# Head 0's mixes at fixed places among the reads of scores, its v loaded behind the next head's q, and the last logarithm ahead of other casts

## The chip, the core and the metric

One NeuronCore of a Trainium2 chip runs the whole program. The time is the device's, in microseconds of one execution. The kernel of before took 965.34, 965.65 and 966.77 us in three runs, a median of 965.65. Its profiled execution took 964.64 us.

A core has five engines, each with its own queue of instructions: TensorE (PE in the profile: matmuls and transposes; PEld is its loading of weights), VectorE (DVE), ScalarE (ACT), GpSimd (POOL) and SyncE (SP, which here only issues DMAs). They meet through semaphores. Matmuls write to banks of PSUM, which DVE and ACT read.

## The reference, cut to what matters

One layer on 1024 tokens of width 1024: norm, a wide projection `w_in`, two groups of heads side by side, a projection `w_out`, norm, residual. The change touches the eight heads of differential attention and the norm of their output:

```python
def block(args):                       # 128 queries, one head
    s = jnp.einsum('bqhmd,bkhmd->bhmqk', qb, k)          # two maps, m = 0, 1
    p = jax.nn.softmax(jnp.where(mask, s, -jnp.inf), axis=-1)
    w = p[:, :, 0] - lam * p[:, :, 1]
    return jnp.einsum('bhqk,bkhv->bqhv', w.astype(v.dtype), v)

oa = diff_attention(qa, ka, va, lam)                     # 8 heads, d = 64, v of 128
oa = rms_norm(oa, subln_g) * (1.0 - lam_init)
oa = oa * jax.nn.silu(ga)
y = jnp.concatenate([oa, ob]) @ w_out                    # ob: the other group
return x + rms_norm(y, post_g)
```

## The kernel before

The in-projection runs first and stores q, k and v of all heads to DRAM (q and k in a high and a low part, from tiles `qk_st`, `qk_hi` and `c`, L482). Attention follows, at about 617 us of the span, and the out-projection is laid between its matmuls: `merge` at the end of the program zips three streams, `all_scores`, `all_values` and `out_early`, by planned costs into one program. A scheduler then orders each engine's instructions by priority and dependence, except those under `tc.keep_in_program_order` (they keep their order among each other) and `tc.issue_after(x)` (behind instruction x).

**Scores.** `scores(h, qb)` makes one block of 128 queries, for `qb` from 7 down to 0, of `n = (qb + 1) * 128` keys. For each of the two maps m it takes the keys in parts of up to 512: PE multiplies q with k and with its low part ks into one of three score banks in rotation (`sc_bank`), and DVE reads the bank, adds the mask, writes the scores to the map's tile (p0 or p1) and their extreme value to `st`. This read is the row `CUSTOM_DVE_ANT_0` of the profile, `ISA` in the lists of the order; the short row behind it fetches the reduced value. In the text a read is named by block and map: block 6's second map has a read of 512 and one of 384 keys. After a map's last read ACT takes the exponential in place with row sums into `st`. After the second map DVE takes the reciprocal of both sums, POOL scales p1 by lambda over its sum, and DVE mixes: `p0 = p0 / sum0 - p1` (`mix_maps`, `SCALAR_TENSOR_TENSOR p<-p,stt,p` in the profile). p0 has a buffer for each block, p1 two in all.

In head 0 the mixes of blocks 7 to 4 are put off: each is put into the list `mixed` and issued behind the last read of the next block, which the scheduler is then free to place. The reciprocals and the reads are free too.

**Values.** `turn` transposes the mixed weights on PE into a bank `wtr`, ACT casts them to `wt_hi`, DVE takes the rest `wt_lo`; `weigh` multiplies them with v into the bank `po` (L142). Head h's v comes in two loads of 512 KB each, by SP (L1243). Head 0's are issued at the program's start of the attention, kept in program order, in tiles taken from the pool `smp` ahead of all others; those of the next heads follow when the head before has ended its first half. q, k and ks of head h + 1 are loaded by SP when head h has reached block 4 (L1127, L1130).

**Norm.** When a half of 512 queries of a head is done, ACT copies `po` to `o`, and `attn_norm` squares (`fold`, `sq`), sums over the 128 rows with a matmul (`ms`), takes logarithm and exponential for the root (`r`), and multiplies with the gate. In the last head the halves are sent directly into the out-projection as the last of its eight groups of rows: the product `gate` is cast to `m_hi` by ACT and the rest `m_lo` by DVE (`last_part`), and PE adds their products to banks `yps`, which have been set to the sums made so far by an ACT copy (`seed`, `yps<-yp`). `mix_pair` casts the groups 4 to 6 of two row blocks (`m_hi<-m_raw`); its second call is held behind `squared_last`.

Of the kernel before, what the change touches and what calls it, by code (L numbers as in the profile page):

```python
# [20 lines left out]
DA_HEADS = 8  # L21
# [10 lines left out]
def hymba_kernel(  # L32
# [1205 lines left out]
    def load_v(h):  # L1238
        v = [smp.tile([P, NT, P], F32R, tag="v", name=f"v{t}", bufs=4) for t in range(2)]
        for t in range(2):  # L1240

            with tc.issue_after(qk_load[0]) if h else nullcontext():
                ins = sp.dma_start(fp(v[t]), v_d[h // 4][h % 4, t])  # L1243
            if h == 0:
                tc.keep_in_program_order(ins)
        return v

    v_first = load_v(0)

    n_sc, n_tr = [0], [0]  # L1250

# [11 lines left out]
    def scores(h, qb):  # L1263

        n = (qb + 1) * P
        qc = slice(qb % 4 * P, qb % 4 * P + P)
        st = const.tile([P, 6], F32, tag="stt", name="stt", bufs=4)
        p0 = pp.tile([P, n], F32, tag=f"p0_{qb}", name="p0", bufs=1 + (qb > 5))
        p1 = smp.tile([P, S], F32, tag="p1", name="p1", bufs=2)
        for m, p in enumerate((p0, p1)):  # L1270
            q = qk[h, "q", qb // 4][:, m, qc]
            parts = parts_of(n)
            if h == DA_HEADS - 1 and (qb, m) in ((1, 1), (0, 0), (0, 1)):

                parts = [(0, 512)]
            for i, (a, b) in enumerate(parts):
                sc = sc_bank("sc", [P, 512])
                for j, name in enumerate(("k", "ks")):
                    for half in range(2):
                        lo, hi = max(a, half * 512), min(b, half * 512 + 512)  # L1280
                        if lo < hi:
                            mm(
                                sc[:, lo - a : hi - a], q,
                                qk[h, name, half][:, m, lo - half * 512 : hi - half * 512],
                                start=(j == 0), stop=(j == 1),
                            )
                e = min(b, n)
                last = i == len(parts) - 1

                behind = tc.issue_after(lowest[0]) if (h, qb) == (0, NT - 2) else nullcontext()  # L1290
                with behind:
                    ins = dve.tensor_tensor_reduce(
                        p[:, a:e], sc[:, : e - a],
                        maskt[:, NZ + P - (e - a) :] if last else maskt[:, : e - a],
                        1.0, 3e38 if i == 0 else st[:, 4 + m : 5 + m], ALU.add, ALU.min,
                        st[:, m : m + 1] if last else st[:, 4 + m : 5 + m],
                    )
                if (h, qb) == (0, NT - 1):
                    lowest[:] = [ins.ins]
                c = 0.08 + (e - a) / 512 * 0.56  # L1300
                if last:
                    act.activation(
                        p[:, :n], p[:, :n], AF.Exp, bias=st[:, m : m + 1], scale=-1.0,
                        accum_out=st[:, 2 + m : 3 + m],
                    )
                if last and m:
                    dve.reciprocal(st[:, 4:6], st[:, 2:4])
                    pool.tensor_scalar(
                        p1[:, :n], p1[:, :n], st[:, 5:6], lam, ALU.mult, ALU.mult
                    )  # L1310
                    while mixed:
                        with tc.issue_after(ins.ins):
                            mixed.pop()()

                    def mix_maps():
                        dve.scalar_tensor_tensor(
                            p0[:, :n], p0[:, :n], st[:, 4:5], p1[:, :n], ALU.mult, ALU.subtract
                        )
                        w[h, qb] = p0

                    if h == 0 and qb > 3:
                        mixed.append(mix_maps)
                    else:
                        mix_maps()
                    c += 0.25 + n / 1024 * 1.4
                yield c

    lowest, mixed = [], []

    def all_scores():  # L1330
        for h in range(DA_HEADS):
            for qb in range(NT - 1, -1, -1):
                if qb in (3, 5) and h:
                    yield lambda h=h, half=qb // 4: (h - 1, half) in used
                yield from scores(h, qb)
                if qb == 4 and h + 1 < DA_HEADS:
                    for n in ("q", "k", "ks"):
                        load_qk(h + 1, n, 1)
                    for n in ("k", "ks"):
                        load_qk(h + 1, n, 0)  # L1340
            if h + 1 < DA_HEADS:
                load_qk(h + 1, "q", 0)
        scored.append(True)
        opened.update(dict.fromkeys(SC))
# [32 lines left out]
                )  # L1377
            n += ns

    def attn_norm(h, half, o):  # L1380
        if h < DA_HEADS - 1:
            gate = smp.tile([P, 512], F32, tag="gate", name="gate", bufs=2)
        else:
            gate = kp.tile([P, 512], F32, tag=("q1", "k1")[half], name="gate")
        with tc.issue_after(qk_load[0]):
            sp.dma_start(gate, g_d[h][:, cols(half)])
        sq = smp.tile([P, 512], F32, tag="r", name="sq", bufs=1)


        hl = smp.tile([P, 512], F32R, tag="sq_hl", name="sq_hl", bufs=1)  # L1390
        fold = smp.tile([P, 512], F32, tag="fold", name="fold", bufs=1)
        act.activation(fold[:64], o[64:], AF.Square)
        ending = h == DA_HEADS - 1 and half
        with tc.issue_after(turned_last[0]) if ending else nullcontext():
            act.activation(sq[:64], o[:64], AF.Square)
        dve.tensor_tensor(sq[:64], sq[:64], fold[:64], ALU.add)
        ins = act.copy(hl[:64], sq[:64]).ins
        if ending:
            squared_last.append(ins)
        dve.tensor_tensor(hl[64:], sq[:64], fp(hl[:64]), ALU.subtract)  # L1400
        if h == DA_HEADS - 1:

            dve.scalar_tensor_tensor(gate, o, sub_g, gate, ALU.mult, ALU.mult)
        for _ in range(4):
            yield 0.0
        n_tr[0] += 1
        ms = bank(TR[n_tr[0] % 2], [P, 512], "ms")
        mm(ms, ones, hl, start=True, stop=True)
        if h == DA_HEADS - 1 and not half:
            opened[TR[n_tr[0] % 2]] = None  # L1410
        r = smp.tile([P, 512], F32, tag="r", name="r", bufs=1)
        act.activation(r, ms, AF.Ln, bias=eps_t, scale=1.0 / P)
        act.activation(r, r, AF.Exp, scale=-0.5)
        if h < DA_HEADS - 1:
            dve.scalar_tensor_tensor(r, o, sub_g, r, ALU.mult, ALU.mult)
            pool.tensor_tensor(gate, r, gate, ALU.mult)
            sp.dma_start(mixd[h * P : (h + 1) * P, cols(half)], gate)
            stored.append(h)
        else:
            dve.tensor_tensor(gate, gate, r, ALU.mult)  # L1420
            last_mix[half] = gate
        yield 0.0

    def all_values():
# [7 lines left out]
        vs, os, turned, norms_todo = {0: v_first}, {}, {}, []  # L1432
        ahead = iter(units)

        def norm_step():
# [6 lines left out]
        for i, (h, half, kts) in enumerate(units):  # L1442
            last = kts[-1] == 4 * half + 3

            ahead_by = AHEAD if h < DA_HEADS - 1 else AHEAD
            while len(turned) < min(i + 1 + ahead_by, len(units)):
                u = next(ahead)
                if u[2] == (0,):
                    yield lambda: (u[0], 4 * u[1]) in w
                turned[u] = turn(*u)  # L1450
                if u[2][-1] == 4 * u[1] + 3:
                    used.add(u[:2])
                yield 0.4
                norm_step()
            if kts == (0,):
                o = smp.tile([P, 512], F32, tag="o", name="o", bufs=3)
                po = bank(PO, [P, 512], "po")
            weigh(po, half, kts, vs[h], turned[h, half, kts])
            norm_step()
            if last:  # L1460
                act.copy(o, po)
                if half and h + 1 < DA_HEADS:
                    vs[h + 1] = load_v(h + 1)
                norms_todo.append(attn_norm(h, half, o))
            yield 0.6

            if i == 1:
                yield SOON * DA_HEADS * 10.0 / T
# [327 lines left out]
```

## Time and profile before

| | us |
|---|---|
| median of three runs | 965.65 |
| the profiled execution | 964.64 |
| its span in the profile | 962.9 |
| PE busy | 953.0 |
| PE's waits for DVE's reads of scores (`sc`), all heads | 0.6 |
| PE's waits for a mix (`wtr`) | 0.4 |
| PE's waits for ACT's `m_hi` at the end | 0.3 |
| PE's waits for DVE's `m_lo` at the end | 0.2 |

The first row of a part of the profile says what its columns are. In a timeline a row begins with the start and the length in us of one instruction (or of a few alike, with their number at the end); brackets at its end give the idle time of that engine just before it, and the engine and the tile that ended the idle time. `p<-sc,maskt,stt 128x512` is an instruction that writes tile `p` from `sc`, `maskt` and `stt`, 128 partitions by 512 elements. Names are without buffer numbers, so `p` stands for p0 and p1.

The time of the profiled execution lies 1.74 us above its span and 1.0 us below the median of the runs.

### The profile page before, as it was taken

The page shows a single profiled execution, that of the slowest core. Times are in us where ns is not written, and L with a number is a line of the kernel's source. Part 1 is how long each engine was busy: PE and PEld are TensorE (multiplying, and loading weights), DVE is VectorE, ACT ScalarE, POOL GpSimd, SP SyncE. Part 2 cuts the span into 40 slices and gives each one's busy share as a digit, 9 for nine tenths or more (in the row PEclk, how much of TensorE's full clock was granted, in tenths as well). Part 3 has the DMA queues.
Part 4 walks back from the last instruction along what each step waited for, and adds up shares of the span by engine and source line. Part 5 has one row for each costly group of instructions (what it writes and reads, how often), then busy time and mean ns, then how long its engine had stood idle before and what let it go on. Part 6 is the DMA issues. An engine that isn't in the chain of part 4 may idle for free.

```text
span 962.9 us, 14404 instructions
## 1 busy us (share of the span) xinstructions
PE 953.0 (99%) x4640; PEld 795.9 (83%) x4640; DVE 736.6 (76%) x1468; ACT 603.6 (63%) x1166; POOL 199.0 (21%) x264
## 2 busy tenths in 40 slices
PE   9999999999999999999999999999999999999997
PEld 7887788888888888888888888878888888888875
DVE  5898799996678687687667576587888888898554
ACT  8753355845677556577765344366777787787773
POOL 3101002122142112111100002122222222433321
PEclk9999999999999999999999999999999999999999
DMA  9616367487577897985754498996666669994767
GB/s 343 217 35 167 91 196 253 163 299 246 189 251 239 281 309 236 299 285 193 259 175 145 151 291 273 408 305 198 219 207 208 220 226 357 320 292 104 162 196 149
DMA packets 152827, 220.36 MB, mean 229 GB/s; under 512 B 15728, under 2 KB 85360, under 8 KB 152656
## 3 DMA queue, kind: packets, MB, share of 16 engines
q1 hardware_dynamic: 138304, 177.65, 57.5%
q0 software_dynamic: 14448, 41.79, 14.9%
q8 instruction: 37, 0.61, 0.3%
q14 instruction: 38, 0.31, 0.1%
HBM read 133.93 MB, written 88.60 MB: 231 GB/s over the span
## 4 chain that ended last, share of the span: by engine, by line
PE 96%; ACT 1%; DVE 1%; DMA 1%; issue 0%; SPq 0%; DVEq 0%; ACTq 0%
PE x L142 24%; PE y L142 16%; PE z L142 16%; PE ypart L142 13%; PE sc L142 7%; PE po L142 5%; PE yps L142 4%; PE wtr L145 3%; PE gpo L142 3%; PE kv L142 1%; PE gkl_ps L142 1%; PE pa L142 1%; DMA x<-in_x_dram 1%; PE xT L145 1%; DVE p L66 1%
## 5 line engine op out<-in xcount | busy, mean ns | idle before, releaser
L66 ACT CAST w<-w_raw 128x512 fp32r<-128x512 f32 x138 | 85.2, 621 | 76.8 <-PE y L142 33.6
L66 DVE TENSOR_TENSOR w<-w_raw,w 128x512 fp32r<-128x512 f32 x138 | 94.1, 685 | 38.4 <-ACT w L66 38.2
L66 ACT ACTIVATE p<-p,stt 128x896 f32<-128x896 f32 (+7 forms) x128 | 99.3, 776 | 34.3 <-DVE stt L66 33.0
L66 ACT COPY s<-x 128x512 f32<-128x512 f32 x78 | 44.8, 587 | 74.2 <-PE x L142 74.0
L66 DVE CUSTOM_DVE_ANT_0 p<-sc,maskt 128x512 f32<-128x512 f32 (+3 forms) x128 | 74.3, 585 | 16.0 <-PE sc L142 14.6
L66 POOL TENSOR_SCALAR p<-p,stt,lam 128x1024 f32<-128x1024 f32 (+3 forms) x64 | 56.4, 882 | 144.8 <-DVE stt L66 144.1
L142 PE MATMUL z<-s_hi,w 128*128 128x512 f32 x320 | 80.2, 393 | 0.0
L142 PE MATMUL x<-s_hi,w 128*128 128x512 f32 x320 | 80.1, 392 | 0.0
L142 PE MATMUL y<-h_hi,w 128*128 128x512 f32 x320 | 80.1, 392 | 0.0
L142 PE MATMUL ypart<-wo_hi,m_hi 128*128 128x512 f32 x192 | 79.5, 414 | 0.1
L142 PE MATMUL ypart<-wo_hi,m_lo 128*128 128x512 f32 x192 | 75.5, 393 | 0.0
L142 PE MATMUL ypart<-wo_lo,m_hi 128*128 128x512 f32 x192 | 75.4, 393 | 0.0
L66 POOL DMA_DIRECT2D wo_d<-wo_hi x32 | 17.4, 544 | 275.0 <-ACT wo_hi L66 275.0
L142 PEld LDWEIGHTS z<-s_hi,w 128*128 128x128 f32 x320 | 59.8, 188 | 12.4
L142 PEld LDWEIGHTS x<-s_hi,w 128*128 128x128 f32 x320 | 59.7, 188 | 12.4
L142 PEld LDWEIGHTS y<-h_hi,w 128*128 128x128 f32 x320 | 59.7, 188 | 12.3
L142 PE MATMUL sc<-k,q 128*128 128x512 f32 (+1 forms) x192 | 68.7, 362 | 0.6 <-DVE stt L66 0.6
L142 PE MATMUL sc<-ks,q 128*128 128x512 f32 (+1 forms) x192 | 66.1, 347 | 0.0
L66 ACT CAST wt_hi<-wtr 128x512 fp32r<-128x512 f32 (+1 forms) x80 | 42.8, 535 | 27.1 <-PE wtr L145 26.1
L66 DVE TENSOR_TENSOR wt_lo<-wtr,wt_hi 128x512 fp32r<-128x512 f32 (+1 forms) x80 | 50.6, 632 | 9.0 <-ACT wt_hi L66 8.5
L66 DVE TENSOR_TENSOR w_raw<-w_raw 128x512 f32<-128x512 f32 x80 | 55.2, 690 | 1.2 <-DMA w_raw<-in_w_in_dram 0.2
L66 DVE TENSOR_TENSOR c<-z,s 128x512 f32<-128x512 f32 x48 | 32.8, 687 | 29.8 <-ACT s L66 19.9
(232 smaller groups left out, 2352.0 us busy)
## 6 DMA issues: line engine op xcount, KB each, us to landing
w_raw<-in_w_in_dram SPq DMA_DIRECT2D x40, 512.0 KB, 5.0
wo_d<-wo_hi POOLq DMA_DIRECT2D x32, 256.0 KB, 3.3
q<-q_d SPq DMA_DIRECT2D x32, 256.0 KB, 4.8
k<-k_d SPq DMA_DIRECT2D x32, 256.0 KB, 5.4
ks<-k_d SPq DMA_DIRECT2D x64, 128.0 KB, 5.9
v<-v_d SPq DMA_DIRECT2D x16, 512.0 KB, 6.5
wo_raw<-in_w_out_dram POOLq DMA_DIRECT2D x31, 256.0 KB, 4.8
wo_d<-gqd POOLq DMA_DIRECT2D x22, 256.0 KB, 4.2
```

What stands on the lines that cost most here:

```text
L66: ins = op(*a, **k)
L142: tc.keep_in_program_order(pe.matmul(*a, **k))
L145: tc.keep_in_program_order(pe.transpose(dst, src, ident))
```

## The change

In head 0 all reads of scores are now kept in program order, and the mixes of blocks 7 to 2 stand at places that a dictionary fixes: block 7's behind the last read of block 5's first map, 6's behind that of block 4's first map, 5's behind block 4's second, 4's behind block 3's second, 3's behind block 1's first, 2's behind block 0's first. Head 0's v loads are no longer issued first and kept in program order; they are taken when head 0 has reached block 4, behind head 1's second-half q. Head 0's `v` tiles are thus taken from their pool behind the tiles of the first blocks, which lie elsewhere than before. At the end `squared_last`, behind which the casts of `mix_pair(2)` stand, is now the exponential of the norm of the last head's second 512 queries instead of the cast to `sq_hl`, and the copy of the last `o` stands behind it too.

```diff
@@ load_v
         for t in range(2):
 
-            with tc.issue_after(qk_load[0]) if h else nullcontext():
-                ins = sp.dma_start(fp(v[t]), v_d[h // 4][h % 4, t])
-            if h == 0:
-                tc.keep_in_program_order(ins)
+            with tc.issue_after(qk_load[0]):
+                sp.dma_start(fp(v[t]), v_d[h // 4][h % 4, t])
         return v
-
-    v_first = load_v(0)
@@ scores
                     lowest[:] = [ins.ins]
+                if h == 0:
+                    tc.keep_in_program_order(ins)
                 c = 0.08 + (e - a) / 512 * 0.56
+                if last and (qb, m) in mixed:
+                    with tc.issue_after(ins.ins):
+                        mixed.pop((qb, m))()
                 if last:
...
-                    while mixed:
-                        with tc.issue_after(ins.ins):
-                            mixed.pop()()
-
                     def mix_maps():
...
-                    if h == 0 and qb > 3:
-                        mixed.append(mix_maps)
+                    if h == 0 and qb > 1:
+                        mixed[(qb - 1, 1) if qb in (4, 5) else (qb - 2, 0)] = mix_maps
                     else:
                         mix_maps()
@@ all_scores
                 if qb == 4 and h + 1 < DA_HEADS:
-                    for n in ("q", "k", "ks"):
+                    load_qk(h + 1, "q", 1)
+                    if not h:
+                        vs[0] = load_v(0)
+                    for n in ("k", "ks"):
                         load_qk(h + 1, n, 1)
@@ attn_norm
-    def attn_norm(h, half, o):
+    def attn_norm(h, half, o, po):
+        if h == DA_HEADS - 1 and not half:
+            with tc.issue_after(squared_last[0]):
+                act.copy(o, po)
...
-        ins = act.copy(hl[:64], sq[:64]).ins
-        if ending:
-            squared_last.append(ins)
+        act.copy(hl[:64], sq[:64])
...
-        act.activation(r, r, AF.Exp, scale=-0.5)
+        ins = act.activation(r, r, AF.Exp, scale=-0.5).ins
+        if ending:
+            squared_last.append(ins)
@@ all_values
             if last:
-                act.copy(o, po)
+                if i + 1 < len(units):
+                    act.copy(o, po)
...
-                norms_todo.append(attn_norm(h, half, o))
+                norms_todo.append(attn_norm(h, half, o, po))
```

The order of instructions on PE and POOL stays as it was. On DVE, in head 0, the rows from block 7's second map (p_5863, now p_5859) to block 6's second map (p_5898, now p_5894) stood like this before, with what each waits for:

```order
L66 ISA p_5863,stt<-sc,maskt,stt 128x512 [waits DVE_49,PE_49]
L66 ISA stt 128x1
L66 ISA p_5897,stt<-sc,maskt 128x512 [waits PE_49]
L66 ISA stt 128x1
L66 ISA p_5897,stt<-sc,maskt,stt 128x384 [waits DVE_49,PE_49]
L66 ISA stt 128x1
L66 RECIPROCAL stt<-stt 128x2 [waits Activation_49]
L66 ISA p_5898,stt<-sc,maskt 128x512 [waits PE_49]
L66 ISA stt 128x1
L66 ISA p_5898,stt<-sc,maskt,stt 128x384 [waits DVE_49,PE_49]
L66 ISA stt 128x1
L66 SCALAR_TENSOR_TENSOR p_5862<-p_5862,stt,p_5863 128x1024 [waits Pool_49]
```

The same place now:

```order
L66 ISA p_5859,stt<-sc,maskt,stt 128x512 [waits DVE_49,PE_49]
L66 ISA stt 128x1
L66 RECIPROCAL stt<-stt 128x2 [waits Activation_49]
L66 ISA p_5893,stt<-sc,maskt 128x512 [waits PE_49]
L66 ISA stt 128x1
L66 ISA p_5893,stt<-sc,maskt,stt 128x384 [waits DVE_49,PE_49]
L66 ISA stt 128x1
L66 ISA p_5894,stt<-sc,maskt 128x512 [waits DMAHW3_49,DMAHW2_49,DMAHW4_49,DMAHW1_49,PE_49]
L66 ISA stt 128x1
L66 ISA p_5894,stt<-sc,maskt,stt 128x384 [waits DVE_49,PE_49]
L66 ISA stt 128x1
L66 RECIPROCAL stt<-stt 128x2 [waits Activation_49]
```

The reciprocal of each block has moved up, from behind the next block's first map to right behind its own block's last read; the mix of block 7 has left this stretch (it now stands behind block 5's first map); and the first read into p_5894 waits for four DMAs.

On ACT, at the end of the attention, before (`ms` is the norm's sum of squares, `m_raw` the raw rows for the casts of `mix_pair(2)`, `yp` the sums made so far):

```order
L66 CAST sq_hl<-sq 64x512
L66 COPY yps<-yp 128x512 x2
L66 CAST m_hi<-m_raw 128x384 x2
L66 COPY yps<-yp 128x512
L66 COPY o<-po 128x512
L66 ACTIVATE r<-ms,eps_t 128x512
L66 ACTIVATE fold<-o 64x512
L66 ACTIVATE r<-r 128x512
L66 ACTIVATE sq<-o 64x512
L66 CAST m_hi<-gate 128x128 x2
```

and now:

```order
L66 CAST sq_hl<-sq 64x512
L66 COPY yps<-yp 128x512 x2
L66 ACTIVATE r<-ms,eps_t 128x512
L66 ACTIVATE r<-r 128x512
L66 COPY o<-po 128x512
L66 CAST m_hi<-m_raw 128x384 x2
L66 COPY yps<-yp 128x512
L66 ACTIVATE fold<-o 64x512
L66 ACTIVATE sq<-o 64x512
L66 CAST m_hi<-gate 128x128 x2
```

The logarithm (`r<-ms,eps_t`) and the exponential (`r<-r`) have passed the copy of `o`, the two casts of `m_raw` and the third copy of `yps`.

On SP, behind the last stores of q in the in-projection, before (`k_6003` and `ks_6006` are head 1's first-half tiles, `k_5995`, `q_5992` and `ks_5998` those of its second half):

```order
L482 DMA q_d<-c 64x512 x2
L1243 DMA v_5846<-v_d 128x1024
L1243 DMA v_5847<-v_d 128x1024
L1127 DMA k_6003<-k_d 128x512 x2
L1130 DMA ks_6006<-k_d 64x512 x4
L1127 DMA k_5995<-k_d 128x512
L1127 DMA q_5992<-q_d 128x512 x2
L1127 DMA k_5995<-k_d 128x512
L1130 DMA ks_5998<-k_d 64x512 x4
```

and now:

```order
L482 DMA q_d<-c 64x512 x2
L1127 DMA k_6003<-k_d 128x512 x2
L1130 DMA ks_6006<-k_d 64x512 x4
L1127 DMA k_5995<-k_d 128x512
L1127 DMA q_5988<-q_d 128x512 x2
L1243 DMA v_5991<-v_d 128x1024
L1243 DMA v_5992<-v_d 128x1024
L1127 DMA k_5995<-k_d 128x512
L1130 DMA ks_5998<-k_d 64x512 x4
```

The two v loads have moved behind nine others.

More of the change, by code (lines that the diff above doesn't have):

```diff
@@ L1326, in scores @@
                 yield c
-    lowest, mixed = [], []
+    lowest, mixed, vs = [], {}, {}
     def all_scores():
@@ L1431, in all_values @@
         ]
-        vs, os, turned, norms_todo = {0: v_first}, {}, {}, []
+        os, turned, norms_todo = {}, {}, []
         ahead = iter(units)
```

## The prediction

> **What bounds the kernel now.** I read the page first, then the chain that ended last, then the stretches around head 0 and the end.
>
> ```profile
> span 962.9 us, 14404 instructions
> PE 953.0 (99%) x4640; PEld 795.9 (83%) x4640; DVE 736.6 (76%) x1468; ACT 603.6 (63%) x1166; POOL 199.0 (21%) x264
> PE 96%; ACT 1%; DVE 1%; DMA 1%; issue 0%; SPq 0%; DVEq 0%; ACTq 0%
> ```
>
> TensorE (PE) is busy for 953.0 of 962.9 us and makes up 96% of the chain. The change neither adds a matmul nor takes one away, and leaves PE's order alone. So it can act only on the moments at which PE waits. The windows over the two places that it touches show how few they are (columns: length, then busy time of PE, PEld, DVE, ACT, POOL, granted clock, DMA share, GB/s):
>
> ```profile
> 630.00:645.00 15.00, 13.98 (x73) 11.24 (x72) 13.01 (x43) 10.48 (x29) 4.75 (x6) 1.00 1.02 319
> 905.00:925.00 20.00, 19.47 (x93) 15.57 (x92) 9.12 (x18) 13.82 (x30) 1.28 (x2) 1.00 0.57 145
> ```
>
> In head 0's softmax PE loses 1.02 us of 15, with VectorE (DVE) busy for 13.01 of them, and at the end 0.53 of 20. PE's timeline shows where head 0 loses it:
>
> ```profile
> 628.52 0.39 PE L142 MATMUL sc<-k,q 128*128 128x256 f32 x1
> 631.80 0.33 PE L142 MATMUL sc<-k,q 128*128 128x128 f32 x1 [0.24 <-DVE stt L66]
> 637.72 0.66 PE L145 MATMUL wtr<-ident,p 128*128 128x128 f32 x4 [0.40 <-DVE p L66]
> 641.91 0.50 PE L142 MATMUL sc<-k,q 128*128 128x512 f32 x1 [0.38 <-DVE stt L66]
> ```
>
> Three PE rows are released by DVE: two by a read of scores (`stt`), one by a mix (`p`). Score banks rotate over three, so a score waits for the read three before it. The brackets are 1.02 us; with the stalled pipe's longer first matmuls and a smaller delay at 628.52 I estimate 2.0 us for all of head 0. That is the most that better places for reads and mixes can bring there.
>
> **Head 0: the mixes move, and so do the reciprocals.** DVE's timeline and ScalarE's (ACT) for the same stretch, before (a row's second column is its length; the instruction behind it starts about 0.08 us before that length is over):
>
> ```profile
> 622.30 0.75 DVE L66 CUSTOM_DVE_ANT_0 p<-sc,maskt,stt 128x512 f32<-128x512 f32 x1
> 624.89 0.16 DVE L66 RECIPROCAL stt<-stt 128x2 f32<-128x2 f32 x1
> 624.97 0.67 DVE L66 CUSTOM_DVE_ANT_0 p<-sc,maskt 128x512 f32<-128x512 f32 x1
> 626.03 0.62 DVE L66 CUSTOM_DVE_ANT_0 p<-sc,maskt,stt 128x384 f32<-128x384 f32 x1 [0.38 <-PE sc L142]
> 626.57 1.28 DVE L66 SCALAR_TENSOR_TENSOR p<-p,stt,p 128x1024 f32<-128x1024 f32 x1
> 627.77 0.68 DVE L66 CUSTOM_DVE_ANT_0 p<-sc,maskt 128x512 f32<-128x512 f32 x1
> 629.18 0.48 DVE L66 CUSTOM_DVE_ANT_0 p<-sc,maskt,stt 128x256 f32<-128x256 f32 x1
> 629.99 1.15 DVE L66 SCALAR_TENSOR_TENSOR p<-p,stt,p 128x896 f32<-128x896 f32 x1
> 632.35 0.33 DVE L66 CUSTOM_DVE_ANT_0 p<-sc,maskt,stt 128x128 f32<-128x128 f32 x1
> 633.55 1.02 DVE L66 SCALAR_TENSOR_TENSOR p<-p,stt,p 128x768 f32<-128x768 f32 x1 [0.59 <-POOL p L66]
> ...
> 623.10 1.15 ACT L66 ACTIVATE p<-p,stt 128x1024 f32<-128x1024 f32 x1 [0.27 <-DVE stt L66]
> 624.15 0.19 ACT L66 ACTIVATION_READ_ACCUMULATOR p<-p,stt 128x1 f32 x1
> 626.69 1.05 ACT L66 ACTIVATE p<-p,stt 128x896 f32<-128x896 f32 x1 [0.54 <-DVE stt L66]
> 630.64 0.92 ACT L66 ACTIVATE p<-p,stt 128x768 f32<-128x768 f32 x1
> 633.55 0.82 ACT L66 ACTIVATE p<-p,stt 128x640 f32<-128x640 f32 x1
> ```
>
> Block 7's last read runs at 622.30. Its exponential runs from 623.10, its row sums are out at 624.34, and the reciprocal of these sums stands two reads later on DVE, at 624.89, where its operand has long been there. The new order has each reciprocal right behind its block's last read, so it waits for ACT, and all the later reads wait behind it. That they do wait, ready or not, is shown by a place in a later head:
>
> ```profile
> 817.84 0.27 PE L142 MATMUL sc<-ks,q 128*128 128x128 f32 x1
> 818.67 0.69 DVE L66 CUSTOM_DVE_ANT_0 p<-sc,maskt 128x512 f32<-128x512 f32 x1 [0.41 <-PE sc L142]
> 819.29 0.29 DVE L66 CUSTOM_DVE_ANT_0 p<-sc,maskt 128x128 f32<-128x128 f32 x1
> ```
>
> The narrow score was finished at 818.11, yet its read ran only at 819.29, behind a read that itself had waited for the score after it. [...]
>
> A second wait is new. Each block's second map goes into one of two buffers `p1`. In the new layout these lie where the stores of q and k out of `qk_st` still read; the first write of block 6's p1 names the last four `q_d<-qk_st` stores. SP's timeline, and the DMA view (KB each, us from issue to landing) of the `k_d` store issued at 609.66 and of the last `q_d` store:
>
> ```profile
> 618.44 3.53 SPq L482 DMA_DIRECT2D q_d<-qk_st  x4
> ...
> k_d<-qk_st SPq DMA_DIRECT2D x1, 128.0 KB, 7.8
> q_d<-qk_st SPq DMA_DIRECT2D x1, 128.0 KB, 5.2
> ```
>
> The four are issued from 618.44 to 621.97, the last at 621.52, so it lands at about 626.7. Before, that read ran at about 625; block 7's p1 waits for `k_d<-qk_st` stores, the last of them issued at 609.66 and landed at 617.5, four us ahead of its first read, which costs nothing.
>
> I walk the new order with these durations, a wake-up of 0.03 to 0.06 us after a wait, and ACT's row sums 0.19 us long:
> - Reciprocal 7 at 624.37; reads of block 6's first map at 624.45 and 625.06; that of its second map waits until 626.77, the next is at 627.38 and done at 628.00. The exponential (1.05, then 0.18) ends at 629.17, reciprocal 6 is at 629.21, block 5's first read at 629.29 instead of 627.77. PE's row of 628.52 waits for it: 630.04, **1.5 late**.
> - Read 629.90, mix 7 (1.28) 630.31, reads 631.51 and 632.12, done 632.60. Exponential (0.92) to 633.66, reciprocal 5 at 633.69, block 4's first read 633.77 to 634.46. PE's row of 631.80: 634.52, **2.7 late**.
> - Read 634.38, mix 6 (1.15) 634.65, reads 635.72 and 636.33, mix 5 (1.02) 636.60, reciprocal 4 at 637.66, reads 637.74 and 638.35, then mix 4 from 638.96 to 639.84. PE's transpose of 637.72 needs it: 639.90, **2.2 late**.
> - From there the order is close to the old one. PE's row of 641.91, the last to be held by DVE, comes at about 644.3.
>
> These delays are one delay, not to be added: head 0 leaves PE **2.4 us later** than before, and the work behind is PE's alone, so nothing gives it back. Its parts: with only the reciprocals' waits the same walk gives +1.7; the store's landing adds the rest, and each us of a later landing adds about 1. Bounds of the unknown: the landing could be up to 1 us earlier (SP's stores come out of a crowded stretch) or 2 later, +1.3 to +4.2; below that only if the reciprocals don't hold the reads. I take +2.4, the landing that the trace shows.
>
> **The v loads.** They issued at 628.84; now they stand behind head 1's first k and ks and both q loads. The rows:
>
> ```profile
> 628.84 1.08 SPq L1243 DMA_DIRECT2D v<-v_d  x2
> v<-v_d SPq DMA_DIRECT2D x4, 512.0 KB, 5.5
> ```
>
> The k and q loads ahead of them wait for PE's late score (634.52), so v issues at about 637 and lands at about 642.5, with 5.5 us. Its first user, the first `po`, ran at 643.15 and comes at about 645.5: 3 us of cover, no cost. The first k and ks go out 1.2 us sooner, which nobody waits for; the last k and ks go out about 1 us later against scores that are 2.4 us later, no cost either. If v came late by more than its cover, each us would be a us.
>
> **The end.** ACT's logarithm and exponential of the last norm pass ahead of the copy `o`, two casts of `m_raw` and a copy of `yps`. ACT's and PE's rows there:
>
> ```profile
> 912.78 0.92 ACT L66 CAST m_hi<-m_raw 128x384 fp32r<-128x384 f32 x2
> 913.61 0.58 ACT L66 COPY yps<-yp 128x512 f32<-128x512 f32 x1
> 914.61 0.68 ACT L66 ACTIVATE r<-ms,eps_t 128x512 f32<-128x512 f32 x1
> 915.97 0.63 ACT L66 ACTIVATE r<-r 128x512 f32<-128x512 f32 x1
> ...
> 912.61 0.50 PE L142 MATMUL ms<-sq_hl,ones 128*128 128x512 f32 x1
> 915.73 0.39 PE L142 MATMUL yps<-wo_hi,m_hi 128*128 128x512 f32 x1
> 917.54 0.39 PE L142 MATMUL yps<-wo_lo,m_hi 128*128 128x512 f32 x1
> 918.97 0.50 PE L142 MATMUL yps<-wo_hi,m_lo 128*128 128x512 f32 x1 [0.23 <-DVE m_lo L66]
> ```
>
> From 915.73 to 917.54 eight matmuls take 1.81 us, 0.23 each. The next two take 1.43 instead of 0.45, waiting for `m_hi` and `m_lo` of the gate: 0.98 lost, some 1.05 with the slower one behind. `ms` ends at 913.11, so the new order runs the logarithm at 913.15 and the exponential from 913.85 to 914.5; the gate's casts follow nearly 1.5 us sooner and are out of the way. But the copy `yps`, which the matmul of 915.73 adds to, now comes behind the `o` copy (0.5) and the casts (0.83): it starts at 915.7 and ends at 916.3, so PE loses about 0.65 at that row instead. Net **-0.4**; bounds -1.05 (the copy in time) and 0.
>
> **The sum.** +2.4 + 0 - 0.4 = **+2.0 us**. The profiled execution took 964.64 us, so 966.6; the median of the three runs is 965.65, 1.0 above it, and the same 2.0 on that gives **967.6**.
>
> **Rivals**, all on the median:
> - *The change does what it says; faster.* The mixes no longer stand between reads, so head 0's 2.0 us of waits go, and 0.4 at the end: 963.3. It needs ACT's sums to be out by the time the reads ahead of each reciprocal are done; it decides from a wait of zero at 623.05, where the walk has 1.3 us. Against it speak the rows of ACT above. 0.12.
> - *Only the reciprocals hold*, the stores landing by 625: +1.7 - 0.4, 967.0, or with the reciprocals' waits partly in the shade of PE's own work +0.9 in all, 966.5. Against it: 626.7 in the trace. 0.18.
> - *A later landing or late loads*: the stores at 627.7 to 628.7, or v's 512 KB behind its cover: +3 to +4 in all, 968.7 to 969.7. For it: DMA share 1.02 in the window. 0.16.
> - *Little moves*: PE's waits only trade places, 965.2 to 965.6. 0.06.
>
> **How the numbers follow.** The forecast (966.8 to 968.4 in its own range) has 0.48. About 0.2%, 1.9 us, is what a measurement of this kernel can tell from no change: same is 963.7 to 967.6. Over half of the forecast lies above that edge (0.29, since what is left out of the walk, the slower first matmuls after a wait, adds), and with the late case (0.16) slower has 0.45. Faster is the first rival, 0.12, and the rest, 0.43, is same. The range goes from 965.0 to 969.6: it leaves out the first rival and the tail of late loads.
>
> **What would show it.** DVE: reciprocal 7 idle for about 1.3 us behind ACT's `p`, the first read of block 6's second map waiting for a DMA until about 626.8, reciprocals 6 and 5 waiting for ACT about 1 us each. PE: the rows of 628.52, 631.80 and 637.72 at about 630.0, 634.5 and 639.9; in the windows 616 to 645 about 2.4 us less busy time. ACT: the copy `yps` of 913.61 ending near 916.3, PE waiting for it, and no wait for the gate's `m_hi`. It would be wrong if the first reads of block 6 came before reciprocal 7, if the store landed at another time, or if the first `po` waited for v.

## The result, and the profile after

| | us | range | runs |
|---|---|---|---|
| before, median | 965.65 | 965.27 to 966.77 | 6 |
| changed, median | 969.35 | 968.73 to 969.98 | 6 |
| profiled execution before / changed | 964.64 / 969.10 | | |
| its span before / changed | 962.9 / 967.4 | | |

The changed kernel takes 1.0037 times as long, with a 95% interval of 1.0025 to 1.0050: slower by 3.7 us between the medians. The prediction was 967.6 within 965.0 to 969.6, so the measured median lies 0.25 us inside the upper bound and outside the narrower 966.8 to 968.4 that was held most likely.

The same two windows as before, of the changed kernel (and the stretch ahead of them; columns as in the prediction):

```profile
616.00:630.00 14.00, 13.71 (x59) 10.36 (x57) 7.67 (x21) 5.10 (x9) 1.19 (x1) 1.00 0.97 355
630.00:645.00 15.00, 11.59 (x52) 8.28 (x53) 11.90 (x34) 8.58 (x21) 3.71 (x4) 1.00 0.73 228
905.00:925.00 20.00, 19.48 (x99) 15.90 (x98) 9.57 (x17) 13.13 (x26) 2.62 (x4) 1.00 0.80 196
```

PE is now idle for 3.41 of the 15 us in which it was idle for 1.02. The end is no worse. PE's waits, total, times and the longest:

```profile
PE sc L142 <- DVE stt L66: 3.2, 5, 1.3
...
PE yps L142 <- ACT yps L66: 0.5, 1, 0.5
```

The waits of scores for DVE's reads went from 0.6 to 3.2 us, and the two waits for the gate's `m_hi` and `m_lo` gave way to one for the copy of `yps`. The rows that the prediction named, on PE's timeline:

```profile
631.26 0.39 PE L142 MATMUL sc<-k,q 128*128 128x256 f32 x1 [1.28 <-DVE stt L66]
636.49 0.33 PE L142 MATMUL sc<-k,q 128*128 128x128 f32 x1 [1.19 <-DVE stt L66]
642.62 0.66 PE L145 MATMUL wtr<-ident,p 128*128 128x128 f32 x4
646.71 0.48 PE L142 MATMUL sc<-k,q 128*128 128x512 f32 x1
```

Head 0's first score started at 618.31 before and at 619.03 here. That is not the change's doing: in the profiles below, which have the same in-projection, the start lies anywhere between 618.31 and 619.56, and at 619.13 in e7, which leaves head 0 as it was. So from here on I compare **stretches**: head 0's, from its first score on PE to head 1's first, is 23.61 us before and 27.68 now; from the first `ms` of the end to the last matmul it is 43.53 and 43.23; what lies between is 270.70 and 270.66. So head 0 costs 4.07, the end gives 0.30, and the sum, 3.77, is close to the 3.7 of the medians. The profiled pair, at 4.46 us, has the later start besides. In three of the changed kernel's six executions the mean granted clock was 0.996 and not 0.999, and their median is 969.93 against 969.10 for the other three; the last section says what that may mean.

Where head 0 lost it, on DVE's timeline of the changed kernel:

```profile
625.15 0.17 DVE L66 RECIPROCAL stt<-stt 128x2 f32<-128x2 f32 x1 [1.36 <-ACT p L66]
625.24 0.67 DVE L66 CUSTOM_DVE_ANT_0 p<-sc,maskt 128x512 f32<-128x512 f32 x1
625.83 0.08 DVE L66 DVE_READ_ACCUMULATOR2_ANT stt<- 128x1 f32 x1
626.06 0.62 DVE L66 CUSTOM_DVE_ANT_0 p<-sc,maskt,stt 128x384 f32<-128x384 f32 x1
626.60 0.08 DVE L66 DVE_READ_ACCUMULATOR2_ANT stt<- 128x1 f32 x1
627.72 0.69 DVE L66 CUSTOM_DVE_ANT_0 p<-sc,maskt 128x512 f32<-128x512 f32 x1 [1.04 <-DMA q_d<-qk_st]
...
630.44 0.17 DVE L66 RECIPROCAL stt<-stt 128x2 f32<-128x2 f32 x1 [1.25 <-ACT p L66]
...
631.76 1.28 DVE L66 SCALAR_TENSOR_TENSOR p<-p,stt,p 128x1024 f32<-128x1024 f32 x1
633.18 0.69 DVE L66 CUSTOM_DVE_ANT_0 p<-sc,maskt 128x512 f32<-128x512 f32 x1
...
635.67 0.17 DVE L66 RECIPROCAL stt<-stt 128x2 f32<-128x2 f32 x1 [1.16 <-ACT p L66]
...
640.40 0.17 DVE L66 RECIPROCAL stt<-stt 128x2 f32<-128x2 f32 x1
```

Three kinds of wait are there. The reciprocals wait 1.36, 1.25 and 1.16 us for ACT's exponential, and the first write of block 6's `p1` waits 1.04 us for the store out of `qk_st`: both foreseen. The third was not: the read of 626.06 starts 0.23 us behind the accumulator row at 625.83 that gives it its starting minimum, with no engine named, and the read of 633.18, which writes the buffer that the mix ahead of it reads, starts 0.14 us after that mix's end.

### The profile page after: what moved, and what is told of

The parts are those of the page before. It is cut to its first block, busy times and chain, and to the rows that moved or that the text cites. A ratio compares the mean times of both kernels' runs of the same rounds, so it can differ in the third digit from the quotient of the medians.

```text
span 967.4 us, 14412 instructions
## 1 busy us (share of the span) xinstructions
PE 954.5 (99%) x4640; PEld 795.9 (82%) x4640; DVE 735.5 (76%) x1468; ACT 604.3 (62%) x1166; POOL 202.2 (21%) x264
## 4 chain that ended last, share of the span: by engine, by line
PE 88%; DVE 5%; DMA 3%; ACT 2%; issue 1%; SPq 0%; DVEq 0%; ACTq 0%
PE x L142 20%; PE y L142 14%; PE z L142 14%; PE ypart L142 13%; PE sc L142 7%; PE po L142 5%; PE yps L142 4%; PE wtr L145 3%; PE gpo L142 3%; PE kv L142 1%; DMA g_raw<-in_w_in_dram 1%; DMA k_d<-qk_st 1%; DVE s_lo L66 1%; PE gkl_ps L142 1%; PE pa L142 1%
```

## The experiments

Each kernel was timed in turn with the kernel before on one chip; the table gives both medians in us, the 95% interval of their ratio, and the two stretches of the kernel's profiled execution. What the stretch of head 0 shows is not the whole loss on the way: before, head 1's first score waits 0.38 us for VectorE; in the changed kernel it does not, and 0.63 us of the loss comes back there. Where it matters I also give the time from the first to the last score of head 0, 22.43 us before and 27.13 in the changed kernel, which is 4.70 longer.

| run | this / before | ratio, 95% | head 0 | end |
|---|---|---|---|---|
| e1, changed, v early | 968.90 / 965.32 | 1.0021 to 1.0046 | 27.70 | 43.19 |
| e2, changed, reciprocals late | 967.34 / 965.32 | 1.0009 to 1.0027 | 25.91 | 43.24 |
| e3, changed, no chained minimum | 967.96 / 965.32 | 1.0018 to 1.0040 | 26.48 | 43.17 |
| e4, changed, reads not pinned | 968.36 / 965.32 | 1.0018 to 1.0041 | 27.21 | 43.17 |
| e5, before, v late | 966.48 / 965.25 | 1.0009 to 1.0026 | 25.07 | 43.53 |
| e6, changed, v early, not pinned | 965.26 / 965.25 | 0.9992 to 1.0010 | 23.94 | 43.19 |
| e7, before, the end | 964.97 / 965.25 | 0.9992 to 1.0009 | 23.64 | 43.20 |
| e8, before, one swap at the end | 964.38 / 965.25 | 0.9985 to 1.0003 | 23.65 | 42.89 |
| e9, before, pins and mixes | 968.06 / 965.10 | 1.0020 to 1.0045 | 26.47 | 43.54 |
| e10, changed, v early, reciprocals late | 965.71 / 965.10 | 1.0000 to 1.0018 | 24.81 | 43.20 |
| e11, e10 without chained minimum | 965.18 / 965.10 | 0.9992 to 1.0009 | 24.11 | 43.22 |
| e12, before, better end | 963.79 / 965.10 | 0.9976 to 0.9994 | 23.68 | 42.38 |

**e1, v early.** Edit of the changed kernel:

```diff
+            with tc.issue_after(qk_load[0]) if h else nullcontext():
+                ins = sp.dma_start(fp(v[t]), v_d[h // 4][h % 4, t])
+            if h == 0:
+                tc.keep_in_program_order(ins)
...
+    v_first = load_v(0)
...
-                    if not h:
-                        vs[0] = load_v(0)
```

> The changed kernel, but head 0's v loads stand first again, as before, so p1 lies where it lay before and its first writes wait for no store. Measure: head 0's stretch on PE, from its first score to head 1's first score, 23.60 us before and 27.68 changed. Theory A (three waits add up on VectorE: reciprocals behind ScalarE, the store's landing, and reads that stand right behind the read or mix whose result they need): the store's share goes, stretch 26.8 to 27.1, time 968.5 to 968.8. Rival (the store's landing hides behind the wait for the reciprocal, which is the whole loss): stretch 27.6, time 969.35, no change. Rival (the v loads' place itself delays the loads of k, q or v): the stretch goes back to about 25, time 967 or less.

The store's wait went, and yet the stretch stayed at 27.70. That would fit the first rival, but PE's rows show another cause. PE's timeline of e1, and its window there:

```profile
636.22 0.63 PE L142 MATMUL ypart<-wo_lo,m_hi 128*128 128x512 f32 x1
636.65 0.63 PE L142 MATMUL ypart<-wo_hi,m_hi 128*128 128x512 f32 x1
637.08 0.63 PE L142 MATMUL ypart<-wo_hi,m_lo 128*128 128x512 f32 x1
```

```profile
636.00:640.00 4.00, 4.00 (x12) 3.16 (x12) 3.59 (x10) 1.50 (x4) 0.65 (x1) 0.62 0.90 271
```

The matmuls are 0.43 us apart instead of 0.23, and the granted clock of the window is 0.62. So e1 could not decide; e9, with the same head 0, was made for it.

**e2, reciprocals late.** The reciprocal and the scaling of `p1` become a closure, issued behind the last read of the next block's first map:

```diff
+                if last and (qb, m) in scaled:
+                    with tc.issue_after(ins.ins):
+                        scaled.pop((qb, m))()
...
-                    dve.reciprocal(st[:, 4:6], st[:, 2:4])
-                    pool.tensor_scalar(
-                        p1[:, :n], p1[:, :n], st[:, 5:6], lam, ALU.mult, ALU.mult
-                    )
+                    if h == 0 and qb > 1:
+                        scaled[qb - 1, 0] = scale_map
+                    else:
+                        scale_map()
```

> The changed kernel, but in head 0 the reciprocal and the scaling of p1 of blocks 7 to 2 stand behind the last read of the next block's first map, reads and mixes as in the change. Theory A: the waits of 1.36, 1.25 and 1.16 us for ScalarE go, the store's wait and the waits on results just written stay: stretch 26.1 to 26.5, time 967.9 to 968.3. Theory B (the reciprocals' place is the whole loss): stretch 23.6 to 24.3, time 965.3 to 966. Rival (the fixed places of the mixes are the loss): stretch 27.4 or more, time 969 to 969.4.

The stretch fell by 1.77 to 25.91, 0.2 below theory A's range, and the time is 0.6 below its range; the reciprocals' place is not the whole loss (theory B), nor is it nothing. From head 0's first to its last score e2 takes 24.25, which is 2.88 less than the changed kernel; e11 below shows why the stretch has less of it. DVE's rows of e2 show what takes over:

```profile
625.09 0.16 DVE L66 RECIPROCAL stt<-stt 128x2 f32<-128x2 f32 x1
627.09 0.69 DVE L66 CUSTOM_DVE_ANT_0 p<-sc,maskt 128x512 f32<-128x512 f32 x1 [1.83 <-DMA q_d<-qk_st]
```

The reciprocal no longer waits, and the store's wait has grown from 1.04 to 1.83 us, since DVE is there earlier.

**e3, no chained minimum.**

```diff
-                        1.0, 3e38 if i == 0 else st[:, 4 + m : 5 + m], ALU.add, ALU.min,
+                        1.0, 3e38 if i == 0 or h == 0 else st[:, 4 + m : 5 + m], ALU.add, ALU.min,
```

> The changed kernel, but in head 0 the read of a map's second part starts its minimum from a constant and not from the first part's minimum, so it no longer waits for the read just before it; what is left out is the first part's minimum in the shift of head 0's exponentials. Theory A with a pause of about 0.2 us for each read right behind the read whose result it takes: six to eight pauses go, some of them in the shade of other waits, stretch 26.5 to 27.0, time 968.2 to 968.7, and the read of a second part follows the first's at 0.61 us instead of 0.83. The walk of the prediction, which had no such pause: at most 0.3 less, 969.05 to 969.35.

The stretch fell by 1.20 to 26.48, just past the good end of theory A's range, and so did the time. The reciprocals' waits are those of the changed kernel; the store's grew from 1.04 to 1.46 us, so the one pause ahead of it was in its shade. On DVE's timeline of e3 the second part follows at 0.60 us:

```profile
624.56 0.67 DVE L66 CUSTOM_DVE_ANT_0 p<-sc,maskt 128x512 f32<-128x512 f32 x1
625.16 0.08 DVE L66 DVE_READ_ACCUMULATOR2_ANT stt<- 128x1 f32 x1
625.16 0.55 DVE L66 CUSTOM_DVE_ANT_0 p<-sc,maskt 128x384 f32<-128x384 f32 x1
```

In the changed kernel it was 0.82 (625.24 to 626.06). The pause of 0.22 us is real and on the path; the walk of the prediction had none. It comes from the dependence and not from the additional operand: in the kernel before, the read of 629.18, which the prediction shows, has the same operand `stt`, stands behind another map's read, and starts together with that read's accumulator row.

**e4, reads not pinned.**

```diff
-                if h == 0:
-                    tc.keep_in_program_order(ins)
```

> The changed kernel, but head 0's reads are not kept in program order; the mixes keep their fixed places. The scheduler then puts reciprocals 7 to 4 where they stood before (two reads later) and lets some reads of the second map pass ahead of a second part. Theory A: the waits for ScalarE go and some of the pauses, the store's wait stays: stretch 24.8 to 25.6, time 966.6 to 967.4. Rival (the mixes' fixed places are the loss): stretch 27 or more, time 969 or more. Rival (the v loads or the store alone are the loss): no change against the changed kernel.

27.21, outside theory A's range, and near the rival's. Again the granted clock fell, to 0.70 in the window from 636 to 640, so this profile does not tell the mixes' places from the clock. The three of its six executions with a mean clock above 0.996 took 967.06, 967.50 and 968.78, too few to tell either. It shows one more thing: mix 7 took 1.91 us, with POOL's scaling of block 6 running beside it (630.55 to 631.64). e5 and e6 take the store and the places apart, and there the clock stayed at 1.00.

**e5, v late alone.** The diff of `load_v` and `all_scores` from the change, on the kernel before.

> The kernel before with the move of head 0's v loads alone. VectorE's order of head 0 stays, but p1 lies on the buffers that the stores of q and k still read. Theory A: the first read of block 6's second map waits for the last q store (about 1.8 us, since no wait for a reciprocal stands ahead of it) and head 0's stretch on PE grows from 23.60 to about 25.0, time 966.5 to 967.0. Rival (the loss needs the reciprocals' waits; the store's landing is covered by slack on VectorE): stretch 23.6 to 24.0, no change. Rival (v late): PE's first po waits, and what it waits for is v.

25.07, theory A. DVE's row of e5:

```profile
627.00 0.69 DVE L66 CUSTOM_DVE_ANT_0 p<-sc,maskt 128x512 f32<-128x512 f32 x1 [1.69 <-DMA q_d<-qk_st]
```

Moving v costs 1.46 us by itself, and none of it by v: it is the buffer that `p1` got instead. No `po` waited for v, here or in the changed kernel.

**e6, mixes' places and the end alone.** The edits of e1 and e4 together.

> The changed kernel without its pinned reads and with head 0's v loads first, as before: of the change only the mixes' fixed places and the end are left. Theory A (pinned reads and the store make the whole loss): stretch 23.3 to 24.0, time 0.0 to 0.6 us under the kernel before. Rival (the mixes' places cost something by themselves): stretch 25 or more, time above the kernel before.

23.94, as theory A has it for the stretch; the time is equal to the kernel before, not under it by the end's 0.3. So with free reads the fixed places cost 0.33 us in the stretch (0.93 at head 0's last score; mix 7 took 1.80 us here, beside POOL), and the rest of the loss needs pinned reads or the store.

**e7, the end alone.** The diff of `attn_norm` and `all_values` from the change, on the kernel before.

> The kernel before with the end's part alone (logarithm and exponential ahead of the o copy, the two casts and the copy of yps). Theory: from the first ms on PE to the last matmul 43.53 before, 43.2 here, as in the changed kernel; the two waits for the gate's m_hi and m_lo go and one for the copy of yps comes; time 0.3 us under the kernel before, which is no measurable change. If the gain were the full cost of the two old waits it would be 1.0.

43.20, as expected; 0.3 us, which the times alone can't tell from nothing.

**e8, one swap at the end.** On the kernel before:

```diff
-        act.activation(fold[:64], o[64:], AF.Square)
+        with tc.issue_after(rooted[0]) if rooted else nullcontext():
+            act.activation(fold[:64], o[64:], AF.Square)
...
-        act.activation(r, r, AF.Exp, scale=-0.5)
+        ins = act.activation(r, r, AF.Exp, scale=-0.5).ins
+        if ending:
+            rooted.append(ins)
```

> The kernel before with one swap on ScalarE at the end: the last half's square (fold) stands behind the exponential of the norm and no longer between logarithm and exponential; the casts and the copy of yps keep their places ahead. The exponential then starts at about 915.3 instead of 916.0 and the gate's cast is done ahead of its need; m_lo may still be about 0.3 late. From the first ms to the last matmul 42.7 to 43.0 us instead of 43.53, time 0.5 to 0.8 under the kernel before. Rival (what ends last at the end is not ScalarE's order): 43.5, no change.

42.89: 0.64 gained in the trace, where the times alone (0.9985 to 1.0003) can't be told from nothing. PE's timeline of e8 names what is late next:

```profile
918.53 0.50 PE L142 MATMUL yps<-wo_hi,m_lo 128*128 128x512 f32 x1 [0.18 <-DVE m_lo L66]
```

**e9, pins and mixes alone.** The changed kernel with v early and the end as before.

> The kernel before with pinned reads and the mixes' fixed places alone (v loads first, end as before): head 0 is that of the run with v early, in which PE's granted clock fell to 0.62 between 636 and 640 us. Theory (the store's wait is part of the loss and the fall of the clock hid its going): where the clock stays at 1.00, head 0's stretch is 26.0 to 26.6 and the time 967.7 to 968.3; where it falls again, 27.4 to 27.8 and 968.9 to 969.3. Rival (the store's landing costs nothing beside the reciprocals): stretch 27.5 or more with the clock at 1.00.

26.47 with the clock at 1.00 all through. Its windows, to be set against e1's 0.62 at the same place:

```profile
630.00:636.00 6.00, 4.28 (x19) 2.93 (x19) 4.41 (x13) 2.54 (x5) 1.33 (x2) 1.00 1.00 331
636.00:640.00 4.00, 3.92 (x17) 2.81 (x17) 3.59 (x10) 2.35 (x6) 0.79 (x1) 1.00 0.91 275
```

So the store adds 1.21 us to the pins (27.68 against 26.47), and the fall of the clock cost e1's profiled execution 1.23.

**e10, both waits out.** The edits of e1 and e2 together.

> The changed kernel with both waits taken out: reciprocals behind the next block's first map, v loads first as before. Left are the reads in program order, each right behind the one whose result it takes, and the mixes' places. Theory A: stretch 24.5 to 25.2 (0.9 to 1.6 over before), and with the end's 0.3 a time 0.6 to 1.3 over the kernel before. Rival (two waits are the whole loss): stretch 23.6, time 0.3 under the kernel before. Rival (waits fill each other's place): stretch as in the run with late reciprocals, 25.9.

24.81, theory A: without the reciprocals' waits and the store's the pinned order is still 1.20 longer than the old one. Of that, 0.73 is there at head 0's last score.

**e11, the pauses out too.** e10 with the edit of e3.

> The run with both waits out, and besides head 0's second parts begin their minimum from a constant (left out: the first part's minimum in the shift of head 0's exponentials), so that the pause between the two reads of a map goes too. Theory A: 0.5 to 0.8 less than with both waits out, stretch 23.8 to 24.4; what is left to 23.6 is the pause behind each mix whose buffer the next read writes. Rival (the pauses lie in the shade of PE): no difference.

24.11: another 0.70. What is left to 23.61 is 0.50, and it is not where the expectation had it, behind the mixes: head 0's last score comes 22.45 us after the first, where it came 22.43 after it before. All of the 0.50 is added at head 1's first score, which waits on PE for a read of DVE. PE's row of e11:

```profile
642.42 0.50 PE L142 MATMUL sc<-k,q 128*128 128x512 f32 x1 [0.86 <-DVE stt L66]
```

In e2 the same score waits 0.87 us, and ahead of that read DVE has stood idle for 0.77 us, at the `wt_lo` of 641.46, which waits for ACT's `wt_hi`. Before, the score waits 0.38 (641.91 in the prediction) and DVE has no such wait; nor has it in the changed kernel and e1. From head 0's last score to head 1's first it is 1.66 us in e2, 1.65 in e10 and 1.66 in e11, against 1.18 before. So I take it, as an estimate, for one and the same cost of the order with late reciprocals, read from e2's rows and taken out by no run, and the new places of the mixes cost nothing in e11.

**e12, a better end.** e8, and besides the norm of the half that comes last (the last head's first 512 queries) is begun behind `early_ends`, its square behind the gate's casts, which `last_cast` collects:

```diff
-        with tc.issue_after(turned_last[0]) if ending else nullcontext():
+        with tc.issue_after(turned_last[0]) if ending else tc.issue_after(last_cast[1]) if len(last_cast) > 1 else nullcontext():
...
-        while len(norms_todo) > 1:
-            norm_step()
-        next(carry)
+        for norm in norms_todo[:-1]:
+            for _ in norm:
+                pass
         yield 0.0
         yield lambda: (ENDS[2], 0) in ps_d
         early_ends()
+        next(carry)
```

> The kernel before with another order at the end: exponential right behind the logarithm, then fold, then the gate's casts m_hi, and the second half's square, sum and cast behind them; the o copy, the casts of m_raw and the copy of yps keep their places ahead. Both old waits of PE go (m_hi and m_lo of the gate, 0.98 us of steps) and none comes: from the first ms to the last matmul 42.4 to 42.7 instead of 43.53, time 0.8 to 1.1 us under the kernel before. Rival (m_lo or the second half's sums are late next): 42.9 or more.

42.38. On ACT the copy of `yps` is ahead, logarithm and exponential are together, and the casts come before the square:

```profile
914.42 0.58 ACT L66 COPY yps<-yp 128x512 f32<-128x512 f32 x1
914.94 0.58 ACT L66 COPY o<-po 128x512 f32<-128x512 f32 x1
915.42 0.69 ACT L66 ACTIVATE r<-ms,eps_t 128x512 f32<-128x512 f32 x1
916.13 0.63 ACT L66 ACTIVATE r<-r 128x512 f32<-128x512 f32 x1
916.79 0.63 ACT L66 ACTIVATE fold<-o 64x512 f32<-64x512 f32 x1
917.52 0.50 ACT L66 CAST m_hi<-gate 128x128 fp32r<-128x128 f32 x2
917.93 0.63 ACT L66 ACTIVATE sq<-o 64x512 f32<-64x512 f32 x1
```

This kernel is faster than the kernel before and than the changed one: 0.9985 of the time before (0.9976 to 0.9994), 1.31 us between the medians, 1.15 of them seen at the end.

## Why it came out slower, step by step

**The bound.** PE's order and work stayed, and only its waits moved: 270.70 and 270.66 us between the two places. Right.

**The reciprocals.** The prediction had waits of 1.3 us and about 1 each; the trace has 1.36, 1.25 and 1.16. Right, and the reads behind them did wait although their scores were there: those of 625.24, 630.52 and 635.75 had been finished on PE at 624.20, 627.48 and 633.60, and each ran 0.08 or 0.09 us behind the start of its reciprocal. So the first rival, with a wait of zero, is out. Taking them out is worth 1.66 of the stretch (e9 to e10) or 1.77 (from the changed kernel, e2), and these figures are low, since e2 and e10 lose about 0.5 of their own at head 1's first score: at head 0's last score it is 2.76 and 2.88.

**The store.** Its last landing was put at about 626.7 with the read behind it at 626.77. Counted from head 0's first score, the read came 8.69 us in against 8.46. Mechanism right. The sum gives it 0.7 (2.4 against 1.7 for the reciprocals alone), but the 1.7 does not come out of the prediction's walk: without the store that read runs at about 625.6, some 1.1 us sooner, and the prediction's own lower bound, with the landing 1 us earlier, is +1.3. So the walk made the store 1.1. It measured 1.21 on top of the pins (e9 to the changed kernel), 1.10 with late reciprocals (e2 to e10) and 1.46 alone (e5).

**The term that was missing.** This is the step of the walk that failed. It said "reads of block 6's first map at 624.45 and 625.06", 0.61 us apart, and took that step for every pair of reads. Where a read starts from the minimum that the read just ahead of it has written, the step is 0.82. The trace of before had shown it, in the row of 622.30 that the prediction quotes: it begins 0.23 us behind this accumulator row of DVE's timeline.

```profile
622.07 0.09 DVE L66 DVE_READ_ACCUMULATOR2_ANT stt<- 128x1 f32 x1
```

The old order put another block's or map's read between many such pairs. Pinning reads in program order put the pairs back to back. Along the changed head 0 that is worth 1.20 us (e3), or 0.70 where the reciprocals' and the store's waits are out (e10 to e11). The walk also let the read behind mix 7 and mix 6 start 0.08 us before the mix is over, as before; in the changed kernel that read writes the buffer which the mix reads, and it starts 0.14 after the mix's end, 0.22 later.

How it adds up can be followed on DVE. Counted from head 0's first score, reciprocals 6, 5 and 4 come 0.51, 1.26 and 2.02 us later than in the walk, and 1.5 of the 2.0 comes in seven steps of some 0.22, one at each of five pairs of reads behind the store and one behind each of the two mixes. On PE the rows of 628.52, 631.80 and 637.72 were 2.0, 4.0 and 4.2 us late, where 1.5, 2.7 and 2.2 were forecast. Of the 1.67 between the forecast's 2.4 for head 0 and the measured 4.07, e3 shows 1.20. The other 0.47 is about what the rows behind the two mixes (0.44) would make; no run took these out with the reciprocals and the store in place, so that part is an estimate.

Put in a row, by the time from head 0's first to its last score and all at a clock of 1.00: 22.43 before, 22.45 with the new places and pinned reads but neither those waits nor the pauses between reads (e11), 23.16 with the pauses (e10), 25.92 with the reciprocals (e9), 27.13 with the store. Of these 4.70, 0.63 comes back at head 1's first score. The shares depend on the order in which they are added: the pauses are 0.70 where DVE has time to spare and 1.20 where the other waits have used it up.

**The v loads.** Forecast to land at about 642.5; the two were issued at 638.17 and 638.64 and landed 6.0 and 7.3 us later, the last at 645.97. The first `po` ran at 647.94 and waited for nothing: 2 us of cover instead of 3, and no cost. Right.

**The end.** Forecast -0.4, measured -0.30 (and -0.33 alone, e7). The row on which it rested, PE behind the copy of `yps`:

```profile
921.10 0.50 PE L142 MATMUL yps<-wo_hi,m_hi 128*128 128x512 f32 x1 [0.52 <-ACT yps L66]
```

PE's step there is 0.91 instead of 0.23, so 0.68 is lost where 0.65 was forecast; the two old waits gave back 0.98 and not 1.05.

**The sum.** The sign, the path and the range held; the point was 1.75 us low, mainly by the missing pauses. That the range held is in part luck: its upper end was there for a later landing of the store or for late v loads. Neither came, and the pauses, which it had not in view, took up that room.

## What to carry to other kernels

Before instructions are pinned in program order, look at what the scheduler had put between a producer and its consumer on one engine: here a foreign read between two dependent ones hid 0.22 us each, and two reads ahead of a reciprocal hid waits of 1.2 to 1.4. A load that is moved changes which buffers the tiles behind it get, and with them whom they wait for; the cost may fall on an instruction that has nothing to do with the load, here 1.46 us of head 0's stretch in e5 and none of it by v. On a path of casts feeding PE, list what PE needs next in order, and put ACT's instructions in that order: e12's end gained 1.15 us where moving one pair ahead of everything gained 0.3.

## What the runs showed of the hardware that was not expected

**The granted clock fell in the middle of the kernel.** In e1 it was 0.62 between 636 and 640 us, with matmuls 0.43 us apart, after waits of PE for head 0's reads of 0.55, 0.34, 0.20 and 1.18 us; e4's profile shows 0.70 at the same place, after a wait of 1.58. In e9, whose head 0 has the same instructions, whose wait ahead of 635.04 was 1.18 too and whose PE was busy for the same 4.28 of the 6 us ahead, it stayed at 1.00, and so it did in the changed kernel's profile, with waits of 1.28, 0.33, 0.20 and 1.19. So the lengths of these waits do not tell in which execution it falls, and no run here shows what does. The mean clock of each timed execution says how often it may have fallen. The profiled executions of e1 and e4, with the fall, have 0.996; all 78 executions of the kernel before that were timed beside e1 to e12 have 0.998 or 0.999. The changed kernel has 0.996 in three of six, so it too seems to fall in some, though not in the profiled one, which has 0.999. The fall cost 1.23 us in e1 (27.70 against e9's 26.47); in the changed kernel's median I estimate a few tenths, from the 969.93 of its three executions at 0.996 against the 969.10 of the others, which no profile shows.

**A read on DVE that used the minimum of the read just ahead of it started after a pause**: 0.23 us from the accumulator's row to the read (625.83 and 626.06 in the changed kernel), against none where it used nothing of it (625.16 in e3, 629.18 before). Behind a mix whose buffer it wrote, the read started 0.14 us after the mix's end (633.18 and 638.15 in the changed kernel); behind one whose buffer it left alone, 0.08 before it (627.77 before, with the mix of 626.57).

**Where a mix and POOL's scaling of a `p1` overlapped in head 0, the one that started second took longer.** Mix 7 took 1.28 us in the kernel before, with POOL idle, but 1.80 and 1.91 us in e6 and e4, where POOL's scaling of block 6 had started 0.37 and 0.25 us ahead of it and took 1.11 and 1.09. In e2 and e10 the mix started first, by about 0.2 us: it took 1.27 and 1.26, and the scaling 2.03 and 2.04 where it takes 1.08 in the changed kernel.
